# Attention with its transposed probabilities in two PSUM banks, each with a copy of its own, and the samples' outputs kept in the second bank

## The chip, the cores and the metric

The kernel runs on one core of a Trainium2 chip. The metric is the device time of one execution in microseconds (us): the median of the timed runs, lower is better. A profile of one further execution records every instruction of the five engines: TensorE (PE for its matmuls, PEld for the loading of their weights), VectorE (DVE), ScalarE (ACT), GpSimd (POOL) and SyncE (SP), which here issues most DMAs. TensorE writes its results to PSUM, eight banks of 512 float32 columns on each of 128 partitions, and ScalarE or VectorE copies them on from there.

## What is computed

One step of a two-layer encoder for a prompt of 1024 frames and 8 samples of 16 frames each. Layer 0 is an RWKV-7 mixing layer, layer 1 an attention layer over a band of frames, and each is followed by a SwiGLU feed-forward part; every part is preceded by an RMS norm with a shift and scale that come from a condition vector. The change is in the attention alone:

```python
def band_attention(q, k_all, v_all, pos0, hist_len, rel_table, qb):
    ...
        s = jnp.einsum('bqhd,bkhd->bhqk', q_b, k_b).astype(jnp.float32) * scale + bias[None]
        s = jnp.where(allowed[None, None], s, NEG_INF)
        p = jax.nn.softmax(s, axis=-1)
        return jnp.einsum('bhqk,bkhd->bqhd', p.astype(v_b.dtype), v_b)
```

There are 16 heads of 64. A prompt frame reads its own chunk of 64 frames and the 8 chunks before it; a sample frame reads 512 cached frames and the 16 new ones.

## The kernel before

**Stages.** The whole program is laid out in one pass, and a scheduler of the language then sets the order of the instructions on each engine: it simulates the program's own timing, takes work in the order in which it was written where that work is ready, and pulls later work forward where it is not. On the chip each engine runs its list strictly in order and waits on semaphores. In time the stages are the RWKV-7 layer, its feed-forward part, the shared keys and values, the attention (about 2436 to 2933 us of the profiled execution), the output projection and the second feed-forward part.

**Attention** (`attention`, line 1630) goes through 8 pairs of heads (`pair`, line 1736). A pair has 16 tiles, one for each of the 8 blocks of 128 prompt queries (`qt`) and each of the two heads (`e`), and two groups of samples, which are put in after the tiles number 1 and 9. Beside these runs a generator of other matmuls, `qgen`: the next pairs' query projections (tile `acc`), and from the seventh pair on a part of the output projection. `advance` (line 1767) is the pipeline written out by hand: the newest tile gets its first and second step, the one before it the third, and the one three before it the last.

**One tile** (`tile`, line 1782) has four steps.
1. Scores: float32 products of queries and keys as two matmuls each into `S`, a PSUM tile of two banks, of which there are two; VectorE takes the row minima (lines 1809 and 1810) and ScalarE the exponentials into `P` in SBUF (line 1811).
2. VectorE divides by the row sums (lines 1813 and 1814).
3. Transposition: `P` has `nk` blocks of 128 keys, 1, 2, 3 and 4 for the first four blocks of queries and 5 for the last four. TensorE transposes each block into a PSUM tile `PT` of two banks (1024 columns, line 1819): the first four blocks lie in the first bank, the fifth in the second. One ScalarE copy takes all of them to `pts` in SBUF (line 1820). `PT` has one buffer, and each tile asks for it anew (line 1817), so that the next tile's transpositions wait until this copy has ended. `pts` has two buffers.
4. Output: for the second head of a pair, matmuls of the values with both heads' `pts` into the PSUM tile `O` of one bank (line 1831, shown under the helper's line 139), which is copied out after every second block of queries (line 1841).

**A group of samples** (`sample_group`, line 1863) does the same for four samples at once: scores, exponentials, five transpositions into `PT` (lines 1894 and 1895) and two copies, of the first bank and of a 16-partition piece of the second (lines 1896 and 1897). Then it asks for `PT` a second time as the accumulator of its outputs (line 1899), scales them to `on` (line 1907), asks for `PT` a third time for the transposition of `on` (lines 1908 and 1909), and VectorE copies that to `so` in two pieces (line 1913). All of these share the one buffer, and so does the next tile.

PSUM is full in this stage: two `S` of two banks, one `PT` of two, `O` and `acc` of one each. A line of the profile at 139 or 268 is that of a helper (`mm`, `split`); the tile's name tells which work it is.

Of the kernel before, what the change touches and what calls it, by code (L numbers as in the profile page):

```python
# [10 lines left out]
AF = mybir.ActivationFunctionType  # L11
# [126 lines left out]
def mm(nc, out, lhsT, rhs, start, stop):  # L138
    return nc.tensor.matmul(out, lhsT, rhs, start=start, stop=stop)  # L139


class Trunk:
# [1115 lines left out]
    def one(self):  # L1258

        self.none = 1 - getattr(self, "none", 0)  # L1260
        return ("O", "acc")[self.none]

# [367 lines left out]
    def attention(self, ctx):  # L1630
        nc, tc = self.nc, self.tc
        at = self.at = self.pp = self.wq = ctx.enter_context(tc.tile_pool(name="att", bufs=1, reuse_waits="tile"))
        self.hw = ("wh", "wl", 3)
        self.halfraw = lambda: self.slot(1)[:, :512]
        self.evt = lambda tag: self.pp.tile([128, 320], F32, tag=tag, name=self.nm(tag), bufs={"xin": 2, "ht": 5}[tag])
        self.qbd = at.tile([128, 4, 2, 16], F32, name="qbd")
        nc.gpsimd.memset(self.qbd, 0.0)
        m1 = self.att("pts", [128, 640], 2)[:, 0:192]
        self.m1r = at.tile([128, 192], F32R, name="m1r")
        nc.gpsimd.memset(m1, 0.0)  # L1640
        nc.gpsimd.memset(m1[0:1, 64:128], 1.0)
        nc.gpsimd.memset(m1[0:1, 128:192], 1e30)
        nc.scalar.activation(self.m1r, m1, AF.Copy)
        self.X, self.xs = {}, {}
        self.O = self.bank("O", 1)
        self.flow = [None] * 3
        for n in range(8):
            if n < 6:
                self.qgen = self.queries(n + 2)
                next(self.qgen, None)  # L1650
            self.qn_ = 2 if n < 6 else 3
            self.pair(n)
            if n < 6:
                for _ in self.qgen:
                    pass
        for _ in self.qgen:
            pass
        rest = self.proj_rest()
        next(rest)
        for _ in range(3):  # L1660
            self.advance(None)
        return rest
# [119 lines left out]
    def tile(self, n, qt, e, vf, bias):  # L1782

        nc = self.nc
        k0 = max(0, qt - 4)
        n0 = max(0, qt - 1)
        nf, nn = (n0 - k0) * 128, (qt + 1 - n0) * 128
        qsl = slice(qt * 128, (qt + 1) * 128)
        nk = qt + 1 - k0
        h = slice(64 * e, 64 * e + 64)  # L1790
        kq = self.KQ[n, e]

        def score(ps, t0, m, mask=False):
            ks = slice(t0 * 128, t0 * 128 + m)
            mm(nc, ps, kq[0][:, qsl], kq[1][:, ks], True, False)
            if mask:
                mm(nc, ps[:, 0:64], self.m1r[:, 0:128], self.m1r[:, 128:192], False, False)
            mm(nc, ps, kq[0][:, qsl], kq[2][:, ks], False, True)


        st = self.att("st", [128, 8], 6)
        P = self.att("P", [128, 640], 3)
        S = self.wide_bank("S", 2)
        if nf:
            score(S[:, 512 - nf:512], k0, nf, qt >= 4)
        near = S[:, 512:512 + nn]
        score(near, n0, nn)
        if nf:
            nc.vector.tensor_reduce(st[:, 0:1], S[:, 512 - nf:512], AX.X, ALU.min)
        nc.vector.tensor_tensor_reduce(near, near, bias[:, 256 - nn:256], 1.0, st[:, 0:1] if nf else 3.0e38, ALU.add, ALU.min, st[:, 1:2])  # L1810
        nc.scalar.activation(P[:, 0:nf + nn], S[:, 512 - nf:512 + nn], AF.Exp, bias=st[:, 1:2], scale=-1.0, accum_out=st[:, 2:3])
        yield
        nc.vector.reciprocal(st[:, 4:5], st[:, 2:3])
        nc.vector.tensor_scalar(P[:, 0:nf + nn], P[:, 0:nf + nn], st[:, 4:5], None, ALU.mult)
        yield
        pts = self.att("pts", [128, 640], 2)
        pt = self.wide_bank("PT", 1)
        for j in range(nk):
            nc.tensor.transpose(pt[:, j * 128:(j + 1) * 128], P[:, j * 128:(j + 1) * 128], self.C("ident"))  # L1819
        nc.scalar.activation(pts[:, 0:nk * 128], pt[:, 0:nk * 128], AF.Copy)  # L1820
        yield
        if not e:
            self.even = pts
            return

        O = self.O[:, qt // 2 % 2 * 256:qt // 2 % 2 * 256 + 256]
        oc = slice(qt % 2 * 128, qt % 2 * 128 + 128)
        for j in range(nk):
            for u, p in enumerate((self.even, pts)):
                hu = slice(64 * u, 64 * u + 64)  # L1830
                mm(nc, O[hu, oc], vf[:, k0 + j, hu], p[:, j * 128:(j + 1) * 128], j == 0, j == nk - 1)
        if qt % 2:
            self.heads_out(n, (qt - 1) * 128, O)

    def heads_out(self, n, t0, O):

# [26 lines left out]
    def sample_group(self, n, g, qs, kn, bt, so):  # L1863
        nc = self.nc
        kc = self.att("kc", [128, 4, 512], 1)
        nc.sync.dma_start(kc, self.a["ck"][n, :, 4 * g:4 * g + 4, :])
        vn = self.att("vn", [16, 4, 128])
        nc.sync.dma_start(vn, self.o["v"][8, g * 64:g * 64 + 64, n * 128:(n + 1) * 128].rearrange("(b t) d -> t b d", t=16))
        vc = self.att("vc", [128, 4, 4, 128], 1)
        nc.sync.dma_start(vc, self.a["cv"][n, :, 4 * g:4 * g + 4])  # L1870
        qbd = self.qbd
        qv = qs.rearrange("p (b t) -> p b t", t=16)
        for e in range(2):
            h = slice(64 * e, 64 * e + 64)
            nc.vector.tensor_copy(qbd[h, :, e, :], qv[h, 4 * g:4 * g + 4, :])
        S = self.wide_bank("S", 2)
        for b in range(4):
            bs = slice(b * 32, b * 32 + 32)
            lq = qbd[:, b].rearrange("p e t -> p (e t)")
            mm(nc, S[bs, 0:512], lq, kc[:, b], True, True)  # L1880
            tb = (4 * g + b) * 16
            mm(nc, S[bs, 512:528], lq, kn[:, tb:tb + 16], True, True)
        st = self.att("st", [128, 8], 6)
        P = self.att("P", [128, 640], 3)
        nc.vector.tensor_reduce(st[:, 0:1], S[:, 0:384], AX.X, ALU.min)
        nc.vector.tensor_tensor_reduce(S[:, 384:528], S[:, 384:528], bt, 1.0, st[:, 0:1], ALU.add, ALU.min, st[:, 1:2])
        nc.scalar.activation(P[:, 0:528], S[:, 0:528], AF.Exp, bias=st[:, 1:2], scale=-1.0, accum_out=st[:, 2:3])
        yield
        nc.vector.reciprocal(st[:, 4:5], st[:, 2:3])
        yield  # L1890
        pts = self.att("pts", [128, 640], 2)
        pt = self.wide_bank("PT", 1)
        for j in range(4):
            nc.tensor.transpose(pt[:, j * 128:(j + 1) * 128], P[:, j * 128:(j + 1) * 128], self.C("ident"))
        nc.tensor.transpose(pt[0:16, 512:640], P[:, 512:528], self.C("ident"))
        nc.scalar.activation(pts[:, 0:512], pt[:, 0:512], AF.Copy)
        nc.scalar.activation(pts[0:16, 512:640], pt[0:16, 512:640], AF.Copy)
        yield
        O = self.wide_bank("PT", 1)
        quarters = [(b, slice(b * 32, b * 32 + 32)) for b in range(4)]  # L1900
        for j in range(4):
            for b, bs in quarters:
                mm(nc, O[bs, 0:128], pts[:, j * 128 + b * 32:j * 128 + b * 32 + 32], vc[:, b, j], j == 0, False)
        for b, bs in quarters:
            mm(nc, O[bs, 0:128], pts[0:16, 512 + b * 32:512 + b * 32 + 32], vn[:, b], False, True)
        on = self.att("on", [128, 128], 1)
        nc.vector.tensor_scalar(on, O[:, 0:128], st[:, 4:5], None, ALU.mult)
        pt = self.wide_bank("PT", 1)
        nc.tensor.transpose(pt[:, 0:128], on, self.C("ident"))
        pv = pt[:, 0:128].rearrange("p (b e t) -> p b e t", b=4, e=2)  # L1910
        for e in range(2):
            h = slice(64 * e, 64 * e + 64)
            nc.vector.tensor_copy(so[h, 4 * g:4 * g + 4, :], pv[h, :, e, :])
        if g == 1:
            self.heads_out(n, 1024, so.rearrange("p b t -> p (b t)"))
# [77 lines left out]
```

## Time and profile before

| | |
|---|---|
| median of 3 runs | 3823.53 us (3821.11 to 3833.7) |
| profiled execution, its own time | 3810.6 us |
| its span from first to last instruction | 3808.8 us |
| granted TensorE clock, mean over the span | 0.944 |
| DVE, ACT, POOL busy | 2282.6, 1574.8, 589.1 us |
| DMA, mean rate | 145 GB/s |

The profiled execution took 13 us less than the median of the timed runs. Its own time is 1.8 us more than its span. Busy time of PE is the union of its matmuls, whose ends are modelled. In the lists of waits a row names the instruction that waited, what ended its wait, the total in us, the number of times and the longest. In the timeline a row has its start and length in us, the engine, the line, the tile it writes and the tiles it reads, the shape, the number of instructions put together in it and, in brackets, the idle time of the engine before the row and what ended it.

### The profile page before, as it was taken

To read this page: it belongs to the slowest core of one execution; us is meant where nothing else is said; L and a number is where in the kernel's file an instruction comes from. 1 tells how busy PE (TensorE), PEld (TensorE's weight loads), DVE (VectorE), ACT (ScalarE), POOL (GpSimd) and SP (SyncE) were. 2 spreads that over 40 slices of the span, in tenths; PEclk is the share of its full clock that TensorE was granted. 3 is DMA by queue.
4 is the path that set the end of the run, shared out by engine and by line. 5 is a ranking of instruction groups with operands and counts; after the bars stand their busy time and mean duration, and the time that the engine had idled before them with its cause. 6 is when DMAs were issued, how large, how long until landed. Compare 5 with 4: busy or idle time off the path is not lost.

```text
span 3808.8 us, 72340 instructions
## 1 busy us (share of the span) xinstructions
PE 3494.9 (92%) x28614; PEld 3089.7 (81%) x28614; DVE 2282.6 (60%) x4484; ACT 1574.8 (41%) x3007; POOL 589.1 (15%) x516
## 2 busy tenths in 40 slices
PE   5789989989899799999999899789889799999999
PEld 3677778777667699999888879677677699999998
DVE  4666667765445855455456742666675755545667
ACT  5545546554223533333311353565654533333310
POOL 0000000000011154443000100000000245544000
PEclk8887899899699899999999999999999899999999
DMA  5776776676665322224655112454564322222521
GB/s 209 235 221 168 206 221 178 194 211 199 189 193 176 124 81 75 76 74 145 221 177 182 69 67 95 148 157 130 156 202 162 113 87 73 76 75 95 172 86 66
DMA packets 426995, 550.87 MB, mean 145 GB/s; under 512 B 128384, under 2 KB 294784, under 8 KB 422176
## 3 DMA queue, kind: packets, MB, share of 16 engines
q1 hardware_dynamic: 351344, 447.53, 36.9%
q0 software_dynamic: 22224, 80.36, 7.0%
q10 hardware_dynamic: 53088, 18.36, 2.1%
q8 instruction: 225, 3.69, 0.4%
q14 instruction: 114, 0.93, 0.1%
HBM read 412.70 MB, written 133.40 MB: 143 GB/s over the span
## 4 chain that ended last, share of the span: by engine, by line
PE 67%; DMA 12%; DVE 10%; ACT 5%; issue 4%; SPq 1%; ACTq 0%; POOL 0%; DVEq 0%; POOLq 0%
PE S L139 32%; PE PT L139 16%; PE acc L139 10%; PE st L139 3%; PE O L139 2%; PE G L139 1%; PE PT L1819 1%; PE aux L139 1%; DVE h L269 1%; DMA TT<-Z 1%; DVE wlo L269 1%; PE Y L139 1%; ACT pts L1820 1%; DMA raw<-in_rw_o 1%; DMA Z<-T 0%
## 5 line engine op out<-in xcount | busy, mean ns | idle before, releaser
L139 PE MATMUL S<-h,w 128*128 128x320 f32 (+1 forms) x4944 | 684.7, 297 | 11.6 <-ACT h L268 3.6
L139 PEld LDWEIGHTS S<-h,w 128*128 128x128 f32 x4944 | 667.9, 190 | 16.8 <-ACT h L268 4.1
L139 PE MATMUL acc<-mx,whi 128*128 128x384 f32 x1728 | 506.0, 370 | 35.9 <-ACT whi L268 14.0
L139 PE MATMUL S<-h,wh 128*128 128x320 f32 (+1 forms) x2844 | 527.8, 337 | 12.0 <-DVE h L1166 5.8
L139 PEld LDWEIGHTS S<-h,wh 128*128 128x128 f32 x2844 | 454.0, 188 | 68.4 <-issue 11.7
L268 ACT ACTIVATE w<-rq 128x512 fp32r<-128x512 f32 x308 | 192.2, 629 | 503.1 <-PE S L139 195.7
L139 PEld LDWEIGHTS acc<-mx,whi 128*128 128x128 f32 x1728 | 335.6, 203 | 68.3 <-ACT whi L268 18.3
L269 DVE TENSOR_TENSOR w<-rq,w 128x512 fp32r<-128x512 f32 x308 | 266.3, 868 | 204.1 <-ACT w L268 203.5
L139 PE MATMUL PT<-h,w 128*128 128x320 f32 (+1 forms) x2448 | 347.1, 297 | 15.5 <-ACT w L268 8.4
L139 PEld LDWEIGHTS PT<-h,w 128*128 128x128 f32 x2448 | 332.5, 190 | 17.4 <-ACT w L268 8.6
L139 PE MATMUL acc<-mx,wlo 128*128 128x384 f32 x864 | 315.0, 365 | 7.7 <-DVE wlo L269 7.7
L139 PE MATMUL PT<-h,wh 128*128 128x320 f32 (+1 forms) x1428 | 287.3, 344 | 11.6 <-DVE wh L269 3.9
L1365 POOL TENSOR_TENSOR t<-t,t 128x576 f32<-128x576 f32 (+1 forms) x132 | 222.2, 1684 | 428.0 <-ACT t L1372 311.3
L139 PEld LDWEIGHTS PT<-h,wh 128*128 128x128 f32 x1428 | 233.7, 190 | 43.1 <-issue 6.0
L139 PEld LDWEIGHTS acc<-mx,wlo 128*128 128x128 f32 x864 | 173.9, 201 | 20.1 <-DVE wlo L269 12.4
L269 DVE TENSOR_TENSOR wlo<-raw,whi 128x1024 fp32r<-128x1024 f32 x114 | 139.0, 1221 | 82.9 <-ACT whi L268 82.0
L269 DVE TENSOR_TENSOR h<-h,h 128x1024 fp32r<-128x1024 f32 (+4 forms) x112 | 122.9, 1111 | 91.5 <-ACT h L268 74.9
L268 ACT ACTIVATE wh<-rq 128x512 fp32r<-128x512 f32 x124 | 74.8, 626 | 242.5 <-PE S L139 160.0
L268 ACT ACTIVATE h<-h 128x1024 fp32r<-128x1024 f32 (+4 forms) x112 | 103.3, 935 | 172.4 <-DMA h<-sd 112.5
L268 ACT ACTIVATE whi<-raw 128x1024 fp32r<-128x1024 f32 x114 | 119.6, 1052 | 123.3 <-PE acc L139 64.0
L1365 DVE TENSOR_TENSOR t<-S,t 128x576 f32<-128x576 f32 (+1 forms) x116 | 86.3, 744 | 126.0 <-PE S L139 125.9
L1432 DVE TENSOR_TENSOR h<-h,S 128x640 f32<-128x640 f32 (+1 forms) x150 | 111.8, 750 | 78.5 <-PE S L139 78.3
(452 smaller groups left out, 5662.3 us busy)
## 6 DMA issues: line engine op xcount, KB each, us to landing
h<-in_wada SPq DMA_DIRECT2D x64, 512.0 KB, 6.1
rq<-in_wg SPq DMA_DIRECT2D x88, 256.0 KB, 2.6
rq<-in_wu SPq DMA_DIRECT2D x88, 256.0 KB, 2.6
rq<-in_wd SPq DMA_DIRECT2D x88, 256.0 KB, 3.0
raw<-in_wada POOLq DMA_DIRECT2D x32, 512.0 KB, 4.5
kc<-in_ck SPq DMA_DIRECT2D x16, 1024.0 KB, 5.0
vc<-in_cv SPq DMA_DIRECT2D x16, 1024.0 KB, 6.1
sd<-t SPq DMA_DIRECT2D x88, 160.0 KB, 1.9
```

The source lines that it names most:

```text
L139: return nc.tensor.matmul(out, lhsT, rhs, start=start, stop=stop)
L268: self.nc.scalar.activation(hi, x, AF.Copy)
L269: self.nc.vector.tensor_tensor(lo, x, hi, ALU.subtract)
L1365: eng.tensor_tensor(out, x, y, ALU.add)
L1432: nc.vector.tensor_tensor(y, y, d, ALU.add)
L1819: nc.tensor.transpose(pt[:, j * 128:(j + 1) * 128], P[:, j * 128:(j + 1) * 128], self.C("ident"))
L1820: nc.scalar.activation(pts[:, 0:nk * 128], pt[:, 0:nk * 128], AF.Copy)
```

## The change

The two banks of `PT` are taken once, at the beginning of the attention, as one lasting tile `self.PT`. A tile of `nk` blocks puts its first three into the first bank and the others, one or two, into the second, and each bank has a copy of its own; tiles with up to three blocks use the first bank and one copy. A group of samples does likewise with three full blocks, then the fourth and the piece of 16 keys, in three copies where there were two. The outputs of the samples are accumulated in the second bank, and `on` is transposed into the second bank.

```diff
-        self.O = self.bank("O", 1)
+        self.O, self.PT = self.bank("O", 1), self.wide_bank("PT", 1)
...
         pts = self.att("pts", [128, 640], 2)
-        pt = self.wide_bank("PT", 1)
-        for j in range(nk):
-            nc.tensor.transpose(pt[:, j * 128:(j + 1) * 128], P[:, j * 128:(j + 1) * 128], self.C("ident"))
-        nc.scalar.activation(pts[:, 0:nk * 128], pt[:, 0:nk * 128], AF.Copy)
+        for i, m in ((0, min(nk, 3)), (3, nk - 3)):
+            if m > 0:
+                pt = self.PT[:, 512:] if i else self.PT
+                for j in range(i, i + m):
+                    nc.tensor.transpose(pt[:, (j - i) * 128:(j - i + 1) * 128], P[:, j * 128:(j + 1) * 128], self.C("ident"))
+                nc.scalar.activation(pts[:, i * 128:(i + m) * 128], pt[:, 0:m * 128], AF.Copy)
         yield
...
         pts = self.att("pts", [128, 640], 2)
-        pt = self.wide_bank("PT", 1)
-        for j in range(4):
-            nc.tensor.transpose(pt[:, j * 128:(j + 1) * 128], P[:, j * 128:(j + 1) * 128], self.C("ident"))
-        nc.tensor.transpose(pt[0:16, 512:640], P[:, 512:528], self.C("ident"))
-        nc.scalar.activation(pts[:, 0:512], pt[:, 0:512], AF.Copy)
-        nc.scalar.activation(pts[0:16, 512:640], pt[0:16, 512:640], AF.Copy)
-        yield
-        O = self.wide_bank("PT", 1)
+        for i, m in ((0, 3), (3, 1)):
+            pt = self.PT[:, 512:] if i else self.PT
+            for j in range(i, i + m):
+                nc.tensor.transpose(pt[:, (j - i) * 128:(j - i + 1) * 128], P[:, j * 128:(j + 1) * 128], self.C("ident"))
+            if i:
+                nc.tensor.transpose(pt[0:16, 128:256], P[:, 512:528], self.C("ident"))
+                nc.scalar.activation(pts[0:16, 512:640], pt[0:16, 128:256], AF.Copy)
+            nc.scalar.activation(pts[:, i * 128:(i + m) * 128], pt[:, 0:m * 128], AF.Copy)
+        yield
+        O = self.PT[:, 512:]
...
-        pt = self.wide_bank("PT", 1)
+        pt = self.PT[:, 512:]
         nc.tensor.transpose(pt[:, 0:128], on, self.C("ident"))
```

## The prediction

> **What bounds the kernel now.** I read the page first (busy time, then the chain that ended last), then the attention's stretch by itself, since the change touches nothing else, then TensorE's waits there.
>
> ```profile
> PE 3494.9 (92%) x28614; PEld 3089.7 (81%) x28614; DVE 2282.6 (60%) x4484; ACT 1574.8 (41%) x3007; POOL 589.1 (15%) x516
> ...
> PE 67%; DMA 12%; DVE 10%; ACT 5%; issue 4%; SPq 1%; ACTq 0%; POOL 0%; DVEq 0%; POOLq 0%
> ```
>
> ```profile
> 2436.00:2933.00 497.00, 436.56 (x3874) 354.88 (x3874) 332.02 (x978) 280.04 (x641) 2.32 (x16) 0.97 0.53 164
> ```
>
> TensorE is the bound of the whole and of this stage: busy 436.6 of 497 us here (columns PE, PEld, DVE, ACT, POOL, granted clock, DMA share, GB/s), ScalarE only 280.0. What the change can give back lies in the 60 us in which TensorE stands still. Its waits in the stage, longest first in total:
>
> ```profile
> PE PT L1819 <- ACT pts L1820: 21.9, 29, 3.2
> PE PT L1819 <- DVE so L1913: 15.3, 11, 4.4
> PE PT L139 <- ACT pts L1820: 6.8, 7, 1.6
> PE PT L1894 <- ACT pts L1820: 3.1, 7, 0.6
> ...
> PE PT L1819 <- ACT pts L1897: 1.9, 1, 1.9
> ```
>
> These five are all waits for the one buffer of `PT`: 49.0 us, nearly the whole of the idle time. Half is a tile's transpositions waiting for the copy of the tile before; 15.3 us is a tile waiting until the samples' transposed outputs have been copied out. So at most some 49 us, 1.3% of the kernel, is within reach. About 0.3%, 11.5 us, is what a measurement of this kernel can tell from no change.
>
> **Part 1: two banks and two copies for a tile.** The usual cycle, two five-block tiles in a row:
>
> ```profile
> 2557.34 0.74 PE L1819 MATMUL PT<-cst,P 128*128 128x128 f32 x5
> ...
> 2558.01 0.43 PE L139 MATMUL O<-pts,vf 128*64 128x128 f32 x2
> ...
> 2558.20 0.69 ACT L1820 ACTIVATE pts<-PT 128x640 f32<-128x640 f32 x1
> ...
> 2558.94 0.33 PE L1819 MATMUL PT<-cst,P 128*128 128x128 f32 x1 [0.50 <-ACT pts L1820]
> ```
>
> The copy starts 0.12 us after the fifth transposition and TensorE goes on 0.05 us after the copy. The prices of the copies by their width:
>
> ```profile
> L1820 ACT ACTIVATE pts<-PT 128x640 f32<-128x640 f32 x64 | 44.7, 699 | 44.9 <-PE PT L1819 38.0 <-PE O L139 6.5
> ...
> L1820 ACT ACTIVATE pts<-PT 128x512 f32<-128x512 f32 x16 | 9.5, 594 | 11.4 <-PE PT L1819 11.3
> ...
> L1820 ACT ACTIVATE pts<-PT 128x384 f32<-128x384 f32 x16 | 7.8, 490 | 6.1 <-PE PT L1819 6.1
> ...
> L1820 ACT ACTIVATE pts<-PT 128x256 f32<-128x256 f32 x16 | 6.0, 374 | 14.0 <-PE PT L1819 13.9
> ...
> L1820 ACT ACTIVATE pts<-PT 128x128 f32<-128x128 f32 x16 | 4.4, 273 | 4.7 <-PE PT L1819 4.6
> ```
>
> Changed, the first copy takes 490 instead of 699 ns and can start two transpositions earlier. Five transpositions span 0.74 us, one alone 0.27 to 0.33, so one more costs about 0.11 us and two 0.22. The first bank is thus free 0.21 + 0.22, say 0.42 us, sooner. The second copy (374 ns) ends about when three transpositions of the next tile are through (0.33 us), so the added wait, of transposition four on the second bank, finds it just free; everything of TensorE is queued behind that wait, and it is covered only by those three transpositions and what the scheduler puts between.
>
> I went through the 29 waits of the first row and the tile before each. Eleven follow a five-block copy at ordinary length, 7.3 us together; in seven of these the copy began at once (saving 0.42 each, 2.9 us), in four ScalarE was late with other work (only the shorter copy counts, 0.21 each, 0.8 us). Three of over 2.6 us each are ScalarE standing before a DMA with the copy queued behind it; they keep all but 0.2 us each (0.6 us). Three follow a four-block copy (0.104 + 0.11, say 0.2 each, 0.6 us). Twelve follow copies of two or three blocks, which don't change. Of the samples' 3.1 us, two waits of 0.49 save 0.42 each and two of 0.61 save 0.21, 1.2 us. Together **6.1 us**.
>
> What it adds is ScalarE time: 490 + 374 - 699 = 165 ns for each of 64 five-block tiles, 490 + 273 - 594 = 169 for each of 16 four-block tiles and for each of 16 sample groups, **16.0 us** of a ScalarE that is busy 280 of 497. The exponentials, the norms of `acc` and the splits of weights are queued behind each second copy, and VectorE and TensorE behind those. The floor of its price is nothing, since ScalarE itself waits for transpositions for far more than that; the ceiling is the whole 16 us. TensorE's waits for `pts` are 33.7 us of the stage, 7%; as these copies sit on just that path I take about a fifth, **3 us**. The Trainium skill says against such a split, in Perfetto Trace Analysis, Optimizing Scalar/DVE Operations, that each operation has a fixed overhead, about 51 ns for ScalarE on PSUM, so that larger ones are better where the engine is saturated; by its figure the addition would be an estimated 96 x 0.051 = 4.9 us instead of 16.0, and the rows (165 ns) decide. The same section says that breaking up instructions may help where ScalarE is not saturated but holds another engine up, which is the state of these rows.
>
> **Part 2: samples' outputs in the second bank alone.** A two-block or three-block tile now never waits for them.
>
> ```profile
> 2464.47 0.41 PE L1819 MATMUL PT<-cst,P 128*128 128x128 f32 x2 [0.94 <-DVE so L1913]
> 2465.36 0.55 PE L1819 MATMUL PT<-cst,P 128*128 128x128 f32 x3 [0.47 <-ACT pts L1820]
> ```
>
> ```profile
> 2871.82 0.74 ACT L268 ACTIVATE h<-h 128x640 fp32r<-128x640 f32 x1 [3.96 <-DMA h<-og]
> ...
> 2874.26 0.66 PE L1819 MATMUL PT<-cst,P 128*128 128x128 f32 x2 [4.35 <-DVE so L1913]
> ```
>
> ```profile
> 2493.79 0.74 PE L1819 MATMUL PT<-cst,P 128*128 128x128 f32 x5 [0.97 <-DVE so L1913]
> 2495.91 0.76 PE L1819 MATMUL PT<-cst,P 128*128 128x128 f32 x5 [1.39 <-ACT pts L1820]
> ```
>
> Of the eleven waits on `so`, seven, 8.9 us, stand before a two-block tile (first and last shown), four, about 6.2 us, before a five-block tile. The seven vanish as such, but behind the one of 4.35 us stands ScalarE, which waits for a DMA until 2872.56 with the next copy behind it: the three-block tile would still wait till about 2873, so that saves 2.4 us and the seven **7 us** (6.6 to 8.9). The waits of about 0.5 us on the two-block copy that follow may shrink since that tile can now be transposed earlier: **1 us** of 2.5. Of the four before five-block tiles only the first three transpositions can go ahead, about 0.4 us each, **1.6 us**; the fourth transposition still waits for `so`. The samples' output matmuls wait for the five-block tile written just before them (6.8 us, third row): they now wait for the second copy, which ends 0.42 - 0.37 = 0.05 us sooner where ScalarE is free and 0.165 later where it isn't: I take **-0.4 us** over seven. The 1.9 us behind the samples' small copy (fifth row) shrinks by about **0.4**.
>
> **Sum.** 6.1 + 7 + 1 + 1.6 + 0.4 - 0.4 - 3 = 12.7 us; I round to 12.5, as a wait that is gone lets the next queue bind a little. Its ends, if nothing of the 16 us lands and the scheduler also fills the four five-block waits, are about 22; if all of the 16 lands, 0. Against the profiled execution: 3810.6 - 12.5 = 3798.1. That execution took 13 us less than the median of the timed runs, 3823.5, which I take as the base: **3811**. What follows the attention is untouched in content; its loads are ahead of it by queue, and a stage that begins 12 us sooner should end so.
>
> **Rivals.** *A: banks are separate in name, but waits are shared.* The samples' copies already read one bank each:
>
> ```profile
> 2809.07 0.60 PE L1894 MATMUL PT<-cst,P 128*128 128x128 f32 x4
> ...
> 2809.51 0.27 PE L1895 MATMUL PT<-cst,P 128*16 128x128 f32 x1
> ...
> 2809.88 0.60 ACT L1896 ACTIVATE pts<-PT 128x512 f32<-128x512 f32 x1 [1.69 <-PE PT L1895]
> ```
>
> ScalarE idles 1.69 us here, and its copy of the first bank starts only after the transposition into the second bank has ended (2809.78), not when the first bank is ready (2809.67). If the changed program's first copy likewise waits for the last transposition, and the next tile likewise for the last copy, the first bank comes free no sooner than before and the last copy 0.165 later: part 1 turns from +6.1 to about -3 (18 waits x 0.165), part 2 stays at 9.6, ScalarE's 3 us stay. That leaves 3 to 4 us, **3820**. For it: this row. Against: in the sample code all transpositions were written before both copies, in the change each copy stands before the next bank's transpositions, so it needs nothing later. Chance 0.22.
>
> *B: the two halves are serialised altogether*, every access to the lasting tile counting as one to both banks. Then transposition four waits for the first copy of its own tile: 0.12 + 0.49 + 0.05 = 0.66 us of TensorE, for 96 groups at most 63 us; half hidden by other matmuls, 32, less the 7 us of part 2 that would vanish with it anyway, so about 25 to 35 us slower, **3850**. It decides from the first tile on: from about 20 groups that stand still for 0.66 us the gain is gone, from 37 it is slower by over 0.3%. For it: the same row; in the trace no engine reads one bank of a tile while another writes its other bank. Against: the code's slices fall exactly on banks, and the hardware asks for no more: in the Trainium skill, PSUM — Partial Sum Buffer, Terms, two engines collide only in the same bank and quadrant. No row here shows two engines in different banks of one tile at once. Chance 0.10.
>
> *C: the scheduler lays out the stage anew*, as freed transpositions are pulled forward in its own timing, and second copies fall behind ScalarE instructions that wait for DMAs. Each such case costs up to 3 us, as the three long ones of part 1 do; four or five cancel the gain, eight make it slower. Chance 0.13, time about **3822**, spread 15 to each side.
>
> **How the numbers follow.** The forecast, 3811, has 0.55; its own range is 3801 to 3823. Faster by over 0.3% (below 3812): 0.55 x 0.65 + 0.22 x 0.1 + 0.13 x 0.25, that is 0.41. Slower by over 0.3% (above 3835): all of B, 0.10, a third of C, 0.04, and 0.04 of the rest, 0.18. Within: 0.41. The range 3799 to 3834 leaves out most of B, the far end of C and the upper end of the gain, together 0.2.
>
> **What would show it.** Right: in the list of TensorE's waits the row on `so` falls from 15.3 to about 6, that on `pts` from 21.9 to 16 to 18; ScalarE's busy time in the stage grows by 16; first copies begin 0.12 us after the third transposition, and the stage is some 12 us shorter. A: first copies begin only after the fifth transposition. B: many waits of 0.6 to 0.7 us inside a tile, between transposition three and four. C: the waits on `PT` fall as forecast, but others, on DMAs or `S`, appear. I am wrong if the `so` row hardly changes, or if the time lost or won lies outside the attention's stretch.

## The result and the profile after

The changed kernel takes **3865.2 us** (median of 6 runs, 3855.57 to 3877.36), the kernel before beside it 3822.32 (6 runs, 3806.82 to 3833.7). The ratio is 1.012 (95% interval 1.0097 to 1.0143): 43 us slower by the medians, 46 by the ratio. Below, a difference is worked out from the ratio, which can be some us off the difference of the medians. The forecast was 3811, with a range of 3799 to 3834. What came is nearest to rival B, which had a chance of 0.10 and a time of 3850.

The profiled execution after has a span of 3853.8 us. First its busy time, then its chain of waits by engine:

```profile
PE 3534.9 (92%) x28614; PEld 3102.7 (81%) x28614; DVE 2290.9 (59%) x4484; ACT 1583.4 (41%) x3103; POOL 594.3 (15%) x516
...
PE 66%; DMA 11%; DVE 9%; issue 7%; ACT 5%; SPq 1%; POOL 0%; ACTq 0%; DVEq 0%; POOLq 0%
```

TensorE has the same 28614 matmuls and is busy 40 us longer; ScalarE has the 96 additional instructions. In the chain only "issue" has grown, from 4 to 7%: time in which an engine waited for nothing that the profile shows. The page alone doesn't tell what happened. The stage does; its windows row after (columns as before: length, the engines' busy time, granted clock, DMA share, GB/s):

```profile
2440.00:2983.00 543.00, 476.56 (x3880) 365.71 (x3878) 332.24 (x967) 287.18 (x731) 2.19 (x15) 0.94 0.49 150
```

Before, the stage lay between 2436 and 2933 us. It begins at the same place and ends 50 us later, at a granted clock of 0.94 where it was 0.97. What comes ahead of it and behind it takes the same time to within 14 us in every trace of this study. TensorE's waits in this stretch after:

```profile
PE PT L1821 <- ACT pts L1822: 26.7, 34, 3.2
...
PE PT L1821 <- DVE so L1917: 9.2, 12, 1.9
PE PT L1821 <- ACT pts L1901: 7.9, 12, 1.8
```

The wait on a tile's copies was to fall from 21.9 to 16 to 18 and rose to 26.7, and the one on the samples' last copy (now that of the fourth block, L1901, before that of the 16 keys, L1897) rose from 1.9 to 7.9. Only the wait on `so` fell, from 15.3 to 9.2, not to 6, and the two rows that stand behind a group of samples are together what they were (17.2 and 17.1). Why, the timeline of a tile of five blocks shows:

```profile
2548.27 0.55 PE L1821 MATMUL PT<-cst,P 128*128 128x128 f32 x3
...
2548.92 0.49 ACT L1822 ACTIVATE pts<-PT 128x384 f32<-128x384 f32 x1
...
2549.85 0.38 PE L1821 MATMUL PT<-cst,P 128*128 128x128 f32 x2
2550.27 0.38 ACT L1822 ACTIVATE pts<-PT 128x256 f32<-128x256 f32 x1 [0.86 <-PE PT L1821]
```

The first copy begins 0.10 us after the third transposition ends, as predicted. But the fourth doesn't go ahead into the free second bank: it comes 0.44 us after that copy has ended, other matmuls having been put between. Where nothing lies between, the trace names the wait:

```profile
2562.32 0.49 PE L1821 MATMUL PT<-cst,P 128*128 128x128 f32 x3
...
2562.93 1.06 ACT L268 ACTIVATE h<-h 128x1024 fp32r<-128x1024 f32 x1 [3.57 <-DMA h<-out_kT]
...
2565.46 0.47 ACT L1822 ACTIVATE pts<-PT 128x384 f32<-128x384 f32 x1
...
2565.99 0.44 PE L1821 MATMUL PT<-cst,P 128*128 128x128 f32 x2 [3.18 <-ACT pts L1822]
```

The row says `pts L1822`, and the only such copy near is that of the tile's own first bank, which ended 0.06 us earlier. TensorE stands 3.18 us ahead of a bank that nobody uses, because ScalarE's copy of the other bank is queued behind a split of keys that waits for its DMA. Of the 560 transpositions of the tiles and the sample groups none begins while a copy from `PT` runs; the earliest follows the end of a copy by 0.05 us. That is turn and turn about: transposition, copy, transposition, copy.

The stage in all traces, worked out from their records. The stage is counted from the first to the last transposition of a tile; idle is the sum of gaps over 80 ns in which neither PE nor PEld runs; "lost" is the stage's length times one minus its mean granted clock, an estimate of what the clock takes:

| kernel | span | stage | TensorE idle | clock | lost |
|---|---|---|---|---|---|
| before | 3808.8 | 490.7 | 59.2 | 0.972 | 13.7 |
| after | 3853.8 | 543.3 | 65.7 | 0.936 | 34.8 |
| two_tiles | 3786.6 | 467.6 | 33.2 | 0.982 | 8.5 |
| copies_last | 3844.7 | 516.3 | 62.1 | 0.939 | 31.4 |
| split_copy | 3841.1 | 515.9 | 61.6 | 0.937 | 32.4 |
| lasting_one_copy | 3813.1 | 493.1 | 58.6 | 0.961 | 19.0 |
| pools_only | 3816.6 | 490.6 | 57.8 | 0.965 | 17.1 |
| extra_act | 3823.8 | 493.6 | 55.8 | 0.951 | 24.4 |
| samples_first | 3802.4 | 480.1 | 41.9 | 0.968 | 15.6 |
| ring | 3780.9 | 452.3 | 26.2 | 0.972 | 12.5 |
| three_turns | 3897.3 | 578.8 | 78.3 | 0.926 | 42.7 |

Of the 52.6 us by which the stage grew, idle time shows only 6.5.

### The profile page after: what moved, and what is told of

It reads as the page before. It is cut to its first block, busy times and chain, and to the rows that moved or that the text cites. A ratio compares the mean times of both kernels' runs of the same rounds, so it can differ in the third digit from the quotient of the medians.

```text
span 3853.8 us, 72487 instructions
## 1 busy us (share of the span) xinstructions
PE 3534.9 (92%) x28614; PEld 3102.7 (81%) x28614; DVE 2290.9 (59%) x4484; ACT 1583.4 (41%) x3103; POOL 594.3 (15%) x516
## 4 chain that ended last, share of the span: by engine, by line
PE 66%; DMA 11%; DVE 9%; issue 7%; ACT 5%; SPq 1%; POOL 0%; ACTq 0%; DVEq 0%; POOLq 0%
PE S L139 32%; PE PT L139 16%; PE acc L139 11%; PE st L139 2%; PE O L139 2%; DMA raw<-in_rw_o 1%; PE PT L1821 1%; DVE h L269 1%; PE G L139 1%; PE aux L139 1%; DMA TT<-Z 1%; DVE wlo L269 1%; DMA vf<-in_wo 1%; PE Y L139 1%; DMA bw<-in_rel 1%
## 5 line engine op out<-in xcount | busy, mean ns | idle before, releaser
L268 ACT ACTIVATE w<-rq 128x512 fp32r<-128x512 f32 x308 | 192.5, 629 | 515.9 <-PE S L139 201.1
L139 PEld LDWEIGHTS PT<-h,w 128*128 128x128 f32 x2448 | 332.3, 190 | 13.7 <-ACT h L268 5.0
```

The source lines that it names most:

```text
L268: self.nc.scalar.activation(hi, x, AF.Copy)
```

## The experiments

All kernels named here compute the whole reference; extra_act has added instructions whose result nobody uses. Theory W: the program's waits are laid by whole PSUM tiles, and the change took one tile of two banks, so the banks take turns. Theory C: ScalarE's additional copies cost the time. Theory R: the lasting tile led the scheduler to another order.

**two_tiles: the change as it is, on two tiles of one bank each.**

```diff
+        self.PT = [self.ptp.tile([128, 512], F32, tag=t, name=self.nm(t), bufs=1) for t in ("PTa", "PTb")]
...
-                pt = self.PT[:, 512:] if i else self.PT
+                pt = self.PT[i > 0]
...
-        O = self.PT[:, 512:]
+        O = self.PT[1]
...
-        pt = self.PT[:, 512:]
+        pt = self.PT[1]
```

The two tiles come from a PSUM pool of their own (`ptp`), which is closed and opened again at both ends of the attention.

> The changed kernel with the two banks as two tiles of one bank each instead of two slices of one tile of two banks; nothing else of the attention differs (PT gets a PSUM pool of its own, opened anew before and after the attention). Theory W (the semaphores are laid by the whole tile: in the changed kernel's trace none of 560 transpositions begins while one of the 256 copies runs): the serial turns vanish, waits are by bank, and the time falls from 3865 to what I forecast for the change itself, 3811, within 3798 to 3826; transpositions of one bank begin while the other bank is copied. Rival C (the price is that of 96 more copies and of the split groups of transpositions, however the waits lie): it stays above 3845.

Measured 3800.9 us, ratio 0.9941 (0.992 to 0.9962): 22 us faster than before, where the change itself is 46 slower, with the same copies in the same number. In its timeline the fourth transposition now begins before the first copy does:

```profile
2525.74 0.55 PE L1833 MATMUL PTa<-cst,P 128*128 128x128 f32 x3
...
2527.02 0.44 PE L1833 MATMUL PTb<-cst,P 128*128 128x128 f32 x2
...
2527.14 0.49 ACT L1834 ACTIVATE pts<-PTa 128x384 f32<-128x384 f32 x1 [0.35 <-PE O L139]
```

TensorE writes `PTb` until 2527.46 while ScalarE reads `PTa` from 2527.14 on. 83 of the 560 transpositions begin while a copy runs, all of them in the tile that this copy does not read. Its waits:

```profile
PE PTa L1833 <- ACT pts L1834: 11.4, 10, 2.2
PE PTb L1833 <- ACT pts L1834: 8.4, 10, 2.0
PE PTb L1833 <- DVE so L1929: 3.3, 3, 1.3
```

The wait on `so` is 3.3 us here. W holds for `PT`, and C can at most be a part.

**pools_only: the kernel before with that pool**, to see what opening it costs.

```diff
+        self.pt_open("ptB")
...
-        return self.ps.tile([128, 1024], F32, tag=tag, name=self.nm(tag), bufs=bufs)
+        return (self.ptp if tag == "PT" else self.ps).tile([128, 1024], F32, tag=tag, name=self.nm(tag), bufs=bufs)
```

> Control for two_tiles: the kernel before, with PT in a PSUM pool of its own that is opened anew before and after the attention. Both theories: as before, 3822, within 3812 to 3832.

Measured 3826.59 us, ratio 1.0015 (0.9993 to 1.0036). The pool gives none of the 22 us.

**lasting_one_copy: the lasting tile and the samples' outputs in its second bank, but one copy a tile as before.** Against the kernel before:

```diff
-        self.O = self.bank("O", 1)
+        self.O, self.PT = self.bank("O", 1), self.wide_bank("PT", 1)
...
-        pt = self.wide_bank("PT", 1)
+        pt = self.PT
...
-        O = self.wide_bank("PT", 1)
+        O = self.PT[:, 512:]
...
-        pt = self.wide_bank("PT", 1)
+        pt = self.PT[:, 512:]
```

The line `pt = self.PT` stands for a tile and for a group of samples alike.

> The kernel before with PT taken once for the whole attention, one copy for a tile as before, the samples' outputs and their transposition in the second bank. Theory W: all accesses share one tile, so the samples' outputs still hold up the next tile: as before, 3822, within 3812 to 3832, the wait of transpositions on so about 15 us. If waits were by bank, the two- and three-block tiles would go free: 3814, and that wait near 6 us. Rival C says as the latter.

Measured 3821.65 us, ratio 0.9995 (0.9982 to 1.0009). Its waits:

```profile
PE PT L1819 <- ACT pts L1820: 21.7, 29, 3.3
PE PT L1819 <- DVE so L1913: 15.2, 12, 4.0
```

They are those of before (21.9 and 15.3), though a tile of two or three blocks and the samples' outputs now share no bank. Part 2 gives nothing on one tile, whatever banks it uses, and the lasting tile by itself costs nothing: R in that form falls.

**copies_last: as the change, but both copies behind all of a tile's transpositions**, which takes the turn inside a tile away and leaves the second copy.

```diff
+        halves = [(i, m, self.PT[:, 512:] if i else self.PT) for i, m in ((0, min(nk, 3)), (3, nk - 3)) if m > 0]
+        for i, m, pt in halves:
+            for j in range(i, i + m):
+                nc.tensor.transpose(pt[:, (j - i) * 128:(j - i + 1) * 128], P[:, j * 128:(j + 1) * 128], self.C("ident"))
+        for i, m, pt in halves:
+            nc.scalar.activation(pts[:, i * 128:(i + m) * 128], pt[:, 0:m * 128], AF.Copy)
```

A group of samples is altered likewise.

> The changed kernel with the order within a tile altered: all of its transpositions into both banks first, then both copies; still one lasting tile. Theory W: the turn inside a tile goes (no copy stands before a transposition of the same tile), what stays is that a tile waits for the last copy of the tile before, which ends 0.165 us later than the one copy did; 3826, within 3815 to 3838. Rival C: copies and their number are the same as in the changed kernel, so above 3845.

Measured 3844.26 us, ratio 1.0044 (1.0024 to 1.0064): 17 us slower than before, more than W said. Its waits in the stage:

```profile
PE O L139 <- ACT pts L1822: 26.9, 23, 5.7
PE PT L1820 <- DVE so L1917: 12.1, 12, 3.7
```

The outputs `O`, which waited 1.0 us for `pts` before, now wait 26.9: in the new order they stand ahead of the next transpositions. The longest:

```profile
2704.41 1.06 ACT L268 ACTIVATE h<-h 128x1024 fp32r<-128x1024 f32 x1 [5.21 <-DMA h<-out_kT]
...
2705.78 0.75 ACT L1822 ACTIVATE pts<-PT 128x384 f32<-128x384 f32 x2
...
2706.31 1.55 PE L139 MATMUL O<-pts,vf 128*64 128x128 f32 x12 [5.71 <-ACT pts L1822]
```

The row of copies holds both of the tile's: the first ends at 2706.26, the second at 2706.53. `O` thus begins 0.05 us after the first copy and 0.22 before the end of the second. So it is with 21 of these 23 waits. The first 12 matmuls of the outputs are those of the tile's first three blocks, and they need only the first copy; that they are ready sooner fits their new place ahead of the next tile's transpositions. The waits on `pts`, a tile in SBUF, thus go by the part that is read, unlike those on `PT`.

So the turn is not the only thing that can cost time on one tile. Two runs followed this up.

**extra_act: the kernel before with 96 instructions on ScalarE that nobody waits for**, one behind the copies of each tile of four or five blocks and of each group of samples.

```diff
+        if nk > 3:
+            nc.scalar.activation(self.idle, self.C("ident")[:, 0:1], AF.Copy)
```

> The kernel before with one more small ScalarE instruction behind the copy of each four- or five-block tile and of each group of samples, 96 in all, some 0.2 us each, of which nobody waits. It prices ScalarE's time alone. My term: a fifth of it lands, 3 to 4 us: 3826, within 3818 to 3834. Rival C: all of it lands, 19 us: 3841 or more.

Measured 3819.82 us, ratio 0.9991 (0.9972 to 1.0011). ScalarE's busy time in the stage rose from 277.5 to 288.6 us, about as much as in the change (287.2), and it cost nothing that can be measured, at most 4 us by the interval. Theory C falls in the form "ScalarE has no time for it".

**split_copy: the kernel before, `PT` taken anew by each tile, only the copy cut in two.**

```diff
-        nc.scalar.activation(pts[:, 0:nk * 128], pt[:, 0:nk * 128], AF.Copy)
+        for i, m in ((0, min(nk, 3)), (3, nk - 3)):
+            if m > 0:
+                nc.scalar.activation(pts[:, i * 128:(i + m) * 128], pt[:, i * 128:(i + m) * 128], AF.Copy)
```

The copy of a group of samples is cut likewise, at column 384.

> The kernel before, with PT taken anew by each tile as there, and only the copy split: the first 384 columns, then the rest, both after all of the tile's transpositions, for the 80 tiles of four and five blocks and the 16 groups of samples. It asks why two copies after all transpositions cost 17 us in the run before of that name. Theory L: the second copy's end, 0.165 us later for each of 96 groups, is waited for by the next tile or by the outputs nearly every time: 96 x 0.165 = 16 us, so about 3838 us (3832 to 3845) beside 3822 for the kernel before, and the granted clock of the stage falls below 0.97. Theory O: the loss came from the order of the instructions that the lasting tile gave, with outputs ahead of the next transpositions: then 3823 us (3817 to 3829), with the waits on PT as before.

Measured 3836.26 us beside 3818.27, ratio 1.0041 (1.0025 to 1.0056): 16 us slower, without a lasting tile. Its waits are those of copies_last:

```profile
PE O L139 <- ACT pts L1822: 27.7, 23, 6.9
PE PT L1819 <- DVE so L1916: 10.3, 11, 2.6
...
PE PT L1819 <- ACT pts L1822: 4.4, 10, 0.6
```

The time is theory L's, 96 x 0.165 us, but its mechanism is not what the trace shows. The two copies of a five-block tile, back to back, take 0.765 us from the first's start to the second's end (median of 64) where the one copy took 0.704: their records overlap by 0.10 us, and the last copy ends 0.06 us later, not 0.165. The next tile's wait on the copies fell from 21.9 to 4.4 us, and the waits on `O` end with the first copy here too. So the cut copy brings the new order even without the lasting tile, and that the time is just 16 us is chance. What is shown is that cutting the copy, on one tile, costs 16 us and needs neither the lasting tile nor the turns; that the order is the cause is argued, as no run held it fixed.

**three_turns: the change with three pieces and three copies for a tile of five blocks**, 64 more turns on the one tile.

```diff
-        for i, m in ((0, min(nk, 3)), (3, nk - 3)):
+        for i, m in ((0, 2), (2, 2), (4, 1)) if nk == 5 else ((0, min(nk, 3)), (3, nk - 3)):
...
-                pt = self.PT[:, 512:] if i else self.PT
+                pt = self.PT[:, 512:] if i in (2, 3) else self.PT
```

> The changed kernel with five blocks as two, two and one, each with its copy: one more serial turn for 64 tiles, a dose of the suspected cost. Theory W: 64 turns at 0.66 us, half hidden, 21 us, and 64 x 0.157 us more of copies: 3888, within 3878 to 3905. Rival C: only the copies and the split groups count, 10 us: 3875 or less.

Measured 3898.25 us, ratio 1.021 (1.0183 to 1.0237), within what was expected. Beside the change's 1.012 that is 0.9%, 34 us more, or 0.53 us for each further turn with its copy. The wait grows with it:

```profile
PE PT L1821 <- ACT pts L1822: 30.5, 39, 4.2
```

**samples_first: two_tiles with the samples' outputs and the transposition of `on` in the first tile**, to price part 2 by itself.

```diff
-        O = self.PT[1]
+        O = self.PT[0]
...
-        pt = self.PT[1]
+        pt = self.PT[0]
```

> two_tiles with the samples' outputs and their transposition in the first tile in place of the second, where the two- and three-block tiles that follow the first group must wait for them. It prices part 2 of the change by itself. Theory W with my term for part 2: 7 to 8 us more than two_tiles, 3808, and the wait on so back above 10 us. Rival: the freed copies of part 1 are all of the gain, 3801.

Measured 3807.23 us, ratio 0.9975 (0.9958 to 0.9991). Between it and two_tiles lie 0.34%, 13 us, with an uncertainty of some 10: part 2 on true tiles. The other 9.6 us (0.25% of 3823, 3 to 16 by the interval) are then part 1's. The sign that was expected in the trace did not come:

```profile
PE PTa L1833 <- ACT pts L1834: 21.3, 21, 4.1
PE PTa L1833 <- DVE so L1929: 3.7, 6, 0.8
```

The wait on `so` did not come back; the wait on `PTa`'s copies doubled. The order is another one, and the row that is named changes with it.

**ring: two buffers of one bank, taken in turn by whatever comes next.** Tiles of up to four blocks are one piece with one copy, five are three and two; the samples' pieces, outputs and transposition take the next bank each.

```diff
+    def half_bank(self):
+        return self.ptp.tile([128, 512], F32, tag="PTr", name=self.nm("PTr"), bufs=2)
...
+        for i, m in ((0, 3), (3, 2)) if nk == 5 else ((0, nk),):
...
+                pt = self.half_bank()
```

> two_tiles with the two one-bank tiles used in turn: up to four blocks in one piece with one copy, five blocks as three and two, and every piece, the samples' outputs and their transposition take whichever bank is next. Theory W: consecutive small tiles no longer wait for each other's copy, and 16 four-block tiles have one copy fewer; some 5 to 8 us off two_tiles (3801): 3795, within 3785 to 3806. Rival D: in turn, the samples' long chain holds up every second piece again, so no gain over two_tiles or a loss: 3801 to 3815.

Measured 3775.87 us, ratio 0.9896 (0.9873 to 0.9919): 40 us faster than before and faster than expected. It is the best version here. Its windows row, and below it what is left of the waits:

```profile
2446.00:2898.00 452.00, 425.37 (x3835) 343.23 (x3835) 315.98 (x962) 280.11 (x714) 3.21 (x15) 0.97 0.57 176
```

```profile
PE PTr L1835 <- ACT pts L1836: 10.7, 11, 3.0
...
PE PTr L139 <- ACT pts L1836: 3.6, 3, 1.2
PE PTr L1835 <- DVE so L1931: 2.5, 4, 0.7
```

Of the 49.0 us that the prediction counted as within reach, these three leave 16.8, and a smaller one on the samples' copies 0.6. Why ring beats two_tiles by another 17 us is only argued: in two_tiles all tiles of up to three blocks follow each other in `PTa`, in ring each takes the bank that the last one left, and 16 copies fewer are made.

## Why the prediction was wrong

**The step that failed** is in part 1: "Changed, the first copy takes 490 instead of 699 ns and can start two transpositions earlier ... The first bank is thus free 0.21 + 0.22, say 0.42 us, sooner". The copy did start two transpositions earlier, but no bank came free by it, because nothing in the program waits for a bank of `PT`. A wait on `PT` belongs to the whole tile, and `self.PT` is one tile. Part 2 rests on the same step: "A two-block or three-block tile now never waits for them" takes it that the bank of the samples' outputs is waited for by itself. The transposition that stands behind the first copy in the program waits for that copy, and the next tile for both. lasting_one_copy shows it without any cut copy, two_tiles by removing it alone, three_turns by adding more of it.

**The evidence was there.** The prediction quoted the sample group's first copy, which waited for a transposition into the other bank, and found that "no engine reads one bank of a tile while another writes its other bank". It then gave the chip's freedom as a reason against B. That reason was of another kind. The Trainium skill (PSUM — Partial Sum Buffer, Terms) tells when two engines collide in PSUM, in the same bank and quadrant; two_tiles agrees, with TensorE in one bank and ScalarE in the other for 0.32 us at 2527.14. It says nothing on which waits a program holds, and those decided.

**Rival A's reason against itself** ("each copy stands before the next bank's transpositions, so it needs nothing later") was right about the copy and is what makes B: the transposition stands behind the copy, so it needs something earlier.

**B's size.** The turn was priced at 0.66 us, half of it hidden, for 96 groups: 25 to 35 us, 3850 for the 3865 that came. Measured are 46 us by the ratio, 0.48 us for each of the 96 groups (0.39 to 0.57), and three_turns adds 0.53 for each further turn (0.3 to 0.7). So about three quarters of the 0.66 us came through, not half. Both prices hold the copy that goes with a turn, and what the turn costs without it is not shown: the 30 us between the change and split_copy are not that price, since the waits on `O`, 27.7 us there, are 1.0 us in the change.

**ScalarE's 3 us** was "about a fifth" of 16.0, and the 16.0 was itself mis-sized. The sum of the records came as forecast: before 85.9 us in all, and after 85.9 + 11.8 + 4.2 = 101.9 (below). But records that stand back to back overlap. ScalarE's busy time in the stage rose by 9.7 us, from 277.5 to 287.2, where 16 was named as a sign, and a cut between copies that follow each other costs 0.06 us, some 6 us for 96; the 4.9 us that the prediction set aside was nearer. ScalarE's time as such is free (extra_act). What the 3 us left out is the order that a cut copy can bring, 16 us in split_copy. How much the copies cost in the change itself is not shown.

```profile
L1822 ACT ACTIVATE pts<-PT 128x384 f32<-128x384 f32 (+2 forms) x208 | 85.9, 413 | 107.8 <-PE PT L1821 89.3 <-PE O L139 14.2 <-DVE st L1810 3.5
L1901 ACT ACTIVATE pts<-PT 128x384 f32<-128x384 f32 (+1 forms) x32 | 11.8, 369 | 7.9 <-PE O L139 7.2 <-PE PT L1897 0.7
L1900 ACT ACTIVATE pts<-PT 16x128 f32<-16x128 f32 x16 | 4.2, 261 | 9.5 <-PE PT L1899 9.5
```

**Part 2** was priced at 7 + 1 + 1.6, 9.6 us; on the one tile it gave nothing (lasting_one_copy), on true tiles about 13. **The sum** of 12.5 us would have been of the right sign and too small for the program that the change's words describe: two_tiles gives 22.

**Rival C** is right in that the order changed: in copies_last and split_copy waits moved to `O`. But the cut copy brings that about, not transpositions pulled forward. Nor is it second copies that fall behind waiting splits: the longest of these waits, 5.71 us, ends with a first copy that stood behind a split waiting for a DMA, as single copies did before (3.2 us).

**The signs of B** were to be waits of 0.6 to 0.7 us between transposition three and four. They are only partly there: the list has 34 waits with 26.7 us for both kinds of turn, since in 90 of the 96 turns other matmuls stand between. Whoever looked for 96 waits in that list would have ruled B out. What shows it is the strict order of transpositions and copies.

**What stays open** is how the 52.6 us of the stage divide. Idle time takes 6.5. The clock takes 34.8 - 13.7 = 21 by the estimate above; but lasting_one_copy, pools_only and extra_act, none of them measurably slower than before, lose 17.1 to 24.4 in their traces, so that it may be only half of that. The rest lies in TensorE's busy time. There the modelled ends hide short waits, since a transposition's record is 0.27 us long where one follows the other every 0.11 us. Counted from the start of one matmul to the start of the next, 37 of the 52.6 us stand at changes from one kind of matmul (the tiles that it writes and reads) to another: 211 us at 849 changes, before 174 us at 711. More changes alone do not do it, as two_tiles has 865 of them in a stage 76 us shorter than the change's. No run held the clock or the order fixed, so the division is not shown.

## What to carry to other kernels

Before a buffer is cut into halves, find out what the program's waits go by: look in the trace for one instruction that works on one half while another engine has the other half, and if there is none, make two tiles of it. A cut copy pays only where the next writer may really go ahead; on one tile it cost 16 us without the turns and 46 with them, and on two tiles the same instructions gained 22. A price that is read off the length of records, like the 0.165 us of a second copy, wants a look at how far records that stand back to back overlap.

## What the runs showed of the hardware

In this stage the records of the granted clock are either 1.0 or 0.5, in stretches of 3.4 us or a multiple of it. Before, 6 stretches at 0.5 begin in the stage, after the change 13, in two_tiles 5. The mean was 0.982 in two_tiles, 0.972 before, 0.936 after and 0.926 in three_turns, with idle time of 33, 59, 66 and 78 us of the stage. The sum of the idle time alone does not set it: from before to after it grows by a ninth and the estimated loss to the clock from 13.7 to 34.8 us, copies_last and split_copy have 62 us of idle time and lose 31 and 32, extra_act has 56 and loses 24, and ring has 26 and loses 12.5 where two_tiles has 33 and loses 8.5. The Trainium skill (TensorE: Matmul & The Clock Gate, A second HAM failure mode: psum-queue depth-cycling) tells of a kernel in which TensorE idles briefly between groups of matmuls, over and over, and the clock goes back and forth between full and half. The trace agrees in that the clock goes back and forth, and more often after the change (0.97 to 0.94); whether the short gaps cause it no run here shows.

And 96 further ScalarE instructions cost nothing that can be measured in a stage in which ScalarE is busy 57% (extra_act, 0.9991), while 96 more copies, in the path from transposition to output, came with 16 us (split_copy). Two copies back to back took 0.765 us where one of the same columns took 0.704.
